# Recurrent gates of a hybrid diffusion backbone: from fp32 matmuls to three fp32r products

## The chip, the cores and the metric

One core of a Trainium2 chip runs the whole forward pass in one launch. The metric is the device time of one execution in microseconds, the median of the runs. The engines are TensorE (PE, with its weight loads as PEld), VectorE (DVE), ScalarE (ACT), GpSimd (POOL) and SyncE (SP), which issues all DMAs of this kernel.

## The reference, cut to what matters

Two layers act on 512 latent tokens and 256 context tokens of width 1024. Each layer projects its input into three head groups, mixes them, projects back, and normalises. The first group is a bidirectional RG-LRU on 384 channels; its two gates are block-diagonal linear maps of the convolved input `u`, in blocks of 64 channels:

```python
def block_diag_linear(u, w, b):
    ub = u.reshape(u.shape[:-1] + (RG_BLOCKS, RG_BLOCK))
    return jnp.einsum('blnd,nde->blne', ub, w).reshape(u.shape) + b

def rglru_scan(u, w_a, b_a, w_x, b_x, lam, h0):
    r = jax.nn.sigmoid(block_diag_linear(u, w_a, b_a))
    i = jax.nn.sigmoid(block_diag_linear(u, w_x, b_x))
    log_a = RG_C * r * jax.nn.log_sigmoid(lam)
    a = jnp.exp(log_a)
    b = jnp.sqrt(-jnp.expm1(2.0 * log_a)) * (i * u)
    ...
```

All inputs and outputs are fp32. The other two groups are a neighbourhood attention and a gated delta rule (GDN).

## The kernel before, in words

Activations lie with channels on partitions and tokens along the free dimension: 256 context columns, then 512 latent columns. A projection (`proj`, L475 to L491) makes 128 output channels: it loads two weight tiles of 128x512 fp32, and multiplies in three fp32r products, high by high, high by low and low by high, 24 matmuls of 512 columns for the latent tokens and 24 of 256 for the context tokens (in layer 1 some leave the context out). The split of a weight tile is `wsplit` (L241): a DMA into a ring of two raw buffers, a ScalarE copy into an fp32r tile `wh` (L237), and a VectorE subtraction into `wl` (L238), both in rings of four, at a raised priority. The input activations are held split as `uh` and `ul`.

The recurrent group has three units `rg(j)` (L1057) of 128 channels in each layer, each a generator whose steps are called in an order written in `CFG["rgord"]`: the projection and convolution that make `u` (tile `rgu`, two buffers); the gate path `za` with SiLU; one step for each direction `d`; and a last step with sqrt, products and scans. A direction's step does four fp32 matmuls at L1071: two gates on 512 latent columns into the PSUM tile `nS`, and two on 256 context columns into `nT`, with the weight tile `rgw`, which one DMA per layer loads whole (128x1536 fp32, 768 KB, L1117 and L1118) when the group's pool is opened. Then ScalarE takes tanh (L1073), exp (L1077) and tanh (L1078), and VectorE the product with `u` (L1080). The last step takes sqrt on ScalarE (L1083, its function table is loaded first), and on VectorE products (L1085, L1086), scans (L1088, L1090), a sum (L1093) and the gate (L1094). `tr` and `ra` have one buffer, `ti` two. The result goes to DRAM (`spill`), or for the unit that ends last straight into the split tiles `uh` and `ul` (`y_in`, L1048 and L1049); the spilled ones are read back by `y_load`.

Beside it, the w_out tiles are loaded and split (L1150, L1151), and the output projection runs at L1177 and L1213. The steps of the groups are interleaved by numbers in `CFG`; within that, a planner at build time lays down each engine's instruction order from priorities and estimated times, and every engine, and SyncE's DMA queue, runs its instructions in that fixed order. A tile's buffer is given out again once all its readers are done.

Of the kernel before, what the change touches and what calls it, by code (L numbers as in the profile page):

```python
# [5 lines left out]
F32 = mybir.dt.float32  # L6
BF16 = mybir.dt.bfloat16
F32R = mybir.dt.float32r
I32 = mybir.dt.int32
AF = mybir.ActivationFunctionType  # L10
ALU = mybir.AluOpType
# [5 lines left out]
NCTX = 256  # L17
NLAT = 512
NTOK = NCTX + NLAT
# [5 lines left out]
CC, CL = 0, 259  # L25
# [114 lines left out]
def _build(tc, I, out, dbg=None):  # L140
    nc = tc.nc
    V, S, G, T = nc.vector, nc.scalar, nc.gpsimd, nc.tensor
    pinned = [False]

    def pin(i):
        return tc.keep_in_program_order(i) if pinned[0] else i

    def dma(**kw):
        return pin(nc.sync.dma_start(**kw))
# [91 lines left out]
    def wsplit(src, n=512):  # L241
        with tc.high_priority(offset=HP):
            return split(raw(src, n), n)
# [226 lines left out]
    for l in range(DEPTH):  # L470
# [586 lines left out]
        def rg(j):  # L1057
            u = rp[0].tile([128, 772], F32, name="rgu", tag="rgu", bufs=2)
# [2 lines left out]
            z = silu_gate(proj("za", j, ctx=not last), "zs")  # L1061
            zdone.append(j)
            yield
            tr = rp[0].tile([128, 2, NTOK], F32, name="tr", tag="tr")
            ti = rp[0].tile([128, 2, NTOK], F32, name="ti", tag="ti", bufs=2)
            a = rp[0].tile([128, 2, NTOK], F32, name="ra", tag="ra")
            for d in range(2):
                for lo, n, at in ((NCTX, NLAT, CL), (0, NCTX, CC)):
                    q = ps("nT", (128, 2, 256)) if lo == 0 else ps("nS", TWO)
                    for g in range(2):  # L1070
                        T.matmul(q[:, g, :n], rp[1][:, j, d, g, :], u[:, at:at + n], start=True, stop=True)  # L1071
                    for g, o in ((0, tr), (1, ti)):
                        S.activation(o[:, d, lo:lo + n], q[:, g, :n], AF.Tanh, scale=0.5,  # L1073
                                     bias=rbh[:, 4 * j + 2 * d + g:4 * j + 2 * d + g + 1])
                L = lh[:, 2 * j + d:2 * j + d + 1]
                L2 = lq[:, 2 * j + d:2 * j + d + 1]
                S.activation(a[:, d], tr[:, d], AF.Exp, scale=L, bias=L)  # L1077
                S.activation(tr[:, d], tr[:, d], AF.Tanh, scale=L2, bias=L2)  # L1078
                for lo, n, at in ((NCTX, NLAT, CL), (0, NCTX, CC)):
                    V.scalar_tensor_tensor(ti[:, d, lo:lo + n], ti[:, d, lo:lo + n], 1.0, u[:, at:at + n],  # L1080
                                           op0=ALU.add, op1=ALU.mult)
                yield
# [9 lines left out]
            c0 = 128 * T0  # L1092
# [8 lines left out]

        P = [na_proj(hp) for hp in range(3)]
        R = [rg(j) for j in range(3)]
        rst = ExitStack()
        rp = [None, None]

        def fill():
            yield from P[0]
            for hp in range(3):
                a = na_att(hp)  # L1110
                if hp < 2:
                    yield from mix(a, P[hp + 1], CFG["mixP"])
                else:
                    yield from a
            nst.close()
            rp[0] = rst.enter_context(tc.tile_pool(name=f"rg{l}", bufs=1, **RW))
            rp[1] = rp[0].tile([128, 3, 2, 2, 128], F32, name="rgw")  # L1117
            dma(out=rp[1].rearrange("p a b c e -> p (a b c e)"), in_=I["rgw"][l])  # L1118
            for ri in CFG["rgord"][l]:
                next(R[ri] if ri < 3 else Z[ri - 3], 0)  # L1120
                yield

        Z = [zg_proj(hp) for hp in range(2)]
        g, f = gdn(), fill()
# [54 lines left out]
        op = ost.enter_context(tc.tile_pool(name=f"op{l}", bufs=1, **RW))  # L1179
# [92 lines left out]
```

## Time and profile before

| | |
|---|---|
| Runs | 886.25, 883.73, 889.57 us; median 886.25 us |
| Profiled execution | 886.25 us, span of the instructions 884.5 us |
| Mean granted TensorE clock | 0.985 of full speed |
| Gate matmuls (L1071) | 96 records for 48 matmuls, in 12 steps |

The span runs from the first to the last instruction of the profiled execution; 1.75 us lie around it. A row of TensorE counts a matmul from its start to a modelled end, and neighbouring matmuls overlap, so their spacing from start to start tells more than their durations. fp32r tiles show as f32 in TensorE's rows.

### The profile page before, as it was taken

What the parts mean: (1) busy time and instruction counts of PE and PEld (TensorE: products, weight loads), DVE (VectorE), ACT (ScalarE), POOL (GpSimd) and SP (SyncE); (2) the same over time, 40 slices, a digit from 0 to 9 for tenths busy, and PEclk for the clock granted to TensorE, in tenths of its full rate; (3) what the DMA queues carried; (4) which work ended last, traced back from release to release, by engine and by line L of the source; (5) the groups of instructions that cost most, each with busy time, mean ns of one, the idle gap of its engine ahead of it and who ended that gap; (6) DMA issues with size and microseconds to landing.
All of it is one profiled execution on the core that took longest, in us unless ns stands there. A gap on an engine that the chain in (4) does not pass through costs nothing.

```text
span 884.5 us, 17982 instructions
## 1 busy us (share of the span) xinstructions
PE 829.5 (94%) x7164; PEld 634.2 (72%) x7164; DVE 680.8 (77%) x1532; ACT 446.7 (51%) x834; POOL 28.9 (3%) x101
## 2 busy tenths in 40 slices
PE   4999999998999999999999999999899899999895
PEld 2676677776777777778677768787676777777674
DVE  2459466797997698759979665899899777877977
ACT  3354443446445245478916644545636544349922
POOL 0000000000000010100001000000000000020001
PEclk9999999999999999999999999999899999999998
DMA  8826633211121110226534172211121211131443
GB/s 311 342 72 227 234 136 132 59 37 31 60 73 62 31 38 3 88 94 205 177 132 173 51 242 89 66 49 49 37 84 60 72 47 65 50 120 57 150 147 122
DMA packets 44901, 94.58 MB, mean 107 GB/s; under 512 B 5249, under 2 KB 10241, under 8 KB 44817
## 3 DMA queue, kind: packets, MB, share of 16 engines
q1 hardware_dynamic: 44816, 93.43, 31.6%
q8 instruction: 56, 0.92, 0.4%
q14 instruction: 29, 0.23, 0.1%
HBM read 84.22 MB, written 9.19 MB: 106 GB/s over the span
## 4 chain that ended last, share of the span: by engine, by line
PE 56%; DVE 22%; ACT 10%; issue 6%; DMA 3%; POOL 1%; SPq 1%; DVEq 0%; POOLq 0%; ACTq 0%
PE pj L489 26%; PE pj L1213 3%; PE nT L985 2%; PE nT L198 2%; DVE wl L238 2%; PE x L846 2%; DVE nsb L977 2%; PE x L198 1%; PE x L1213 1%; PE gab L198 1%; PE nS L198 1%; DVE ti L1090 1%; PE nS L590 1%; ACT wh L237 1%; ACT dgc L738 1%
## 5 line engine op out<-in xcount | busy, mean ns | idle before, releaser
L489 PE MATMUL pj<-uh,wh 128*128 128x512 f32 (+1 forms) x680 | 246.2, 362 | 0.0
L489 PE MATMUL pj<-ul,wh 128*128 128x512 f32 (+1 forms) x680 | 242.8, 357 | 0.0
L489 PE MATMUL pj<-uh,wl 128*128 128x512 f32 (+1 forms) x680 | 242.2, 356 | 0.0
L489 PEld LDWEIGHTS pj<-uh,wh 128*128 128x128 f32 x680 | 129.8, 191 | 22.8 <-issue 7.3
L489 PEld LDWEIGHTS pj<-ul,wh 128*128 128x128 f32 x680 | 129.9, 191 | 16.9 <-issue 3.2
L489 PEld LDWEIGHTS pj<-uh,wl 128*128 128x128 f32 x680 | 129.9, 191 | 14.2 <-issue 0.9
L238 DVE TENSOR_TENSOR wl<-raw,wh 128x512 fp32r<-128x512 f32 (+1 forms) x106 | 71.8, 680 | 44.3 <-ACT wh L237 44.0
L237 ACT ACTIVATE wh<-raw 128x512 fp32r<-128x512 f32 (+1 forms) x106 | 65.7, 623 | 70.8 <-PE pj L489 67.6
L981 ACT ACTIVATE nsb<-nsb,mx 128x512 f32<-128x512 f32 x48 | 34.5, 720 | 30.5 <-DVE mx L979 30.1
L987 ACT ACTIVATE ptb<-nT 128x512 f32<-128x512 f32 (+1 forms) x60 | 33.4, 557 | 26.0 <-PE nT L985 25.5
L985 PE MATMUL nT<-cst,nsb 128*128 128x128 f32 x216 | 36.8, 287 | 4.9 <-ACT ptb L987 3.5
L543 DVE SCALAR_TENSOR_TENSOR cs<-xp,tph,cs 128x771 f32<-128x771 f32 (+1 forms) x36 | 35.0, 973 | 2.8 <-ACT cs L541 2.2
L985 PEld LDWEIGHTS nT<-cst,nsb 128*128 128x128 f32 x216 | 23.8, 142 | 16.5 <-ACT ptb L987 7.3
L198 PE MATMUL nT<-ptb,vt 128*64 128x128 f32 x432 | 31.1, 285 | 3.4 <-ACT ptb L987 3.4
L828 ACT ACTIVATE sb<-vtm 64x256 f32<-64x256 f32 x48 | 19.6, 413 | 23.7 <-DVE sb L839 14.0
L752 DVE TENSOR_TENSOR ln<-ln,tmp 128x60 f32<-128x60 f32 (+14 forms) x60 | 30.2, 503 | 1.2
L198 PEld LDWEIGHTS nT<-ptb,vt 128*64 128x64 f32 x432 | 23.7, 140 | 10.2 <-ACT ptb L987 9.3
L750 DVE TENSOR_TENSOR tmp<-ln 128x60 f32<-128x60 f32 (+14 forms) x60 | 30.0, 501 | 1.0
L198 PE MATMUL nS<-kT,qT 64*128 64x512 f32 (+1 forms) x180 | 26.9, 403 | 1.0 <-DVE mx L977 0.9
L1226 ACT ACTIVATE lsq<-rr,mv 128x1024 bf16<-128x1024 f32 x10 | 11.7, 1166 | 30.8 <-DVE mv L1224 30.8
L539 ACT ACTIVATE xp<-pj 128x512 f32<-128x512 f32 (+1 forms) x30 | 14.7, 488 | 21.8 <-PE pj L489 18.0
L977 DVE CUSTOM_DVE_ANT_1 nsb<-nS,bt 128x512 f32<-128x512 f32 x36 | 24.4, 685 | 1.4 <-ACT ptb L987 0.7
(300 smaller groups left out, 1668.3 us busy)
## 6 DMA issues: line engine op xcount, KB each, us to landing
raw<-in_win SPq DMA_DIRECT2D x104, 256.0 KB, 2.6
wm<-in_wmod SPq DMA_DIRECT2D x48, 512.0 KB, 5.6
raw<-in_wout SPq DMA_DIRECT2D x32, 256.0 KB, 2.8
bt<-in_rpb SPq DMA_DIRECT2D x18, 256.0 KB, 2.7
xt<-in_x SPq DMA_DIRECT2D x12, 256.0 KB, 7.8
xr<-in_x SPq DMA_DIRECT2D x12, 256.0 KB, 2.5
xpd<-xo SPq DMA_DIRECT2D x12, 256.0 KB, 2.0
yd<-zs SPq DMA_DIRECT2D x6, 384.0 KB, 3.0
```

The costliest lines, as they stand in the source:

```text
L198: return lambda: T.matmul(o, a, b, start=start, stop=stop)
L237: S.activation(h[:, :n], t[:, :n], AF.Copy)
L238: V.tensor_tensor(out=l[:, :n], in0=t[:, :n], in1=h[:, :n].bitcast(F32), op=ALU.subtract)
L489: T.matmul(q[:, :n], a[:, sl], b[:, bl_, kc, :], start=k == 0, stop=k == 23)
L543: V.scalar_tensor_tensor(o, x[:, lo_ + k:k + NCONV], taps[:, k:k + 1], o, op0=ALU.mult, op1=ALU.add)
L750: V.tensor_tensor(out=tv, in0=ln[:, :, k + 1:32, k:k + 1].to_broadcast([128, 2, n, k]), in1=ln[:, :, k:k + 1, 0:k].to_broadcast([128, 2, n ...
L752: V.tensor_tensor(out=ln[:, :, k + 1:32, 0:k], in0=ln[:, :, k + 1:32, 0:k], in1=tv, op=ALU.add)
L977: V.tensor_tensor_reduce(sb.rearrange("p (a b) -> p a b", a=2), p_[:, h2].rearrange("p (a b) -> p a b", a=2), bias, 1.0, -3e38, op0=ALU.ad ...
L981: S.activation(sb[:, 0:128 * nk], src, AF.Exp, bias=mx[:, 0, b, h2:h2 + 1], accum_out=mx[:, 1, b, h2:h2 + 1])
L985: T.transpose(pt[:, g, :], sb[:, 128 * g:128 * g + 128], ident)
L987: S.activation(t_[:, 0:nk], pt[:, 0:nk], AF.Copy)
L1213: T.matmul(q, a[:, t, kc, :], b, start=k == 0, stop=k == 23)
```

## The change

The gates' matmuls take split operands. Each unit splits its 128x512 part of the gate weights with `wsplit`, that is, through the raw, `wh` and `wl` rings of the projections, and splits `u` into two fp32r tiles `ruh` and `rul` with one buffer each, by a ScalarE copy and a VectorE subtraction for the latent and for the context columns. Each fp32 matmul becomes three fp32r ones that accumulate in PSUM. The tile `rgw` and its load are gone; the two new tiles take the same 6 KB per partition.

```diff
@@ -1061,6 +1061,11 @@
             z = silu_gate(proj("za", j, ctx=not last), "zs")
             zdone.append(j)
             yield
+            wh, wl = wsplit(I["rgw"][l][:, 512 * j:512 * j + 512])
+            uu = [rp[0].tile([128, NTOK], F32R, name="ru" + a, tag="ru" + a) for a in "hl"]
+            for lo, n, at in ((NCTX, NLAT, CL), (0, NCTX, CC)):
+                S.activation(uu[0][:, lo:lo + n], u[:, at:at + n], AF.Copy)
+                V.tensor_tensor(out=uu[1][:, lo:lo + n], in0=u[:, at:at + n], in1=uu[0][:, lo:lo + n].bitcast(F32), op=ALU.subtract)
             tr = rp[0].tile([128, 2, NTOK], F32, name="tr", tag="tr")
             ti = rp[0].tile([128, 2, NTOK], F32, name="ti", tag="ti", bufs=2)
             a = rp[0].tile([128, 2, NTOK], F32, name="ra", tag="ra")
@@ -1068,7 +1073,9 @@
                 for lo, n, at in ((NCTX, NLAT, CL), (0, NCTX, CC)):
                     q = ps("nT", (128, 2, 256)) if lo == 0 else ps("nS", TWO)
                     for g in range(2):
-                        T.matmul(q[:, g, :n], rp[1][:, j, d, g, :], u[:, at:at + n], start=True, stop=True)
+                        c0 = 256 * d + 128 * g
+                        for i, (a_, b_) in enumerate(((wh, uu[0]), (wh, uu[1]), (wl, uu[0]))):
+                            T.matmul(q[:, g, :n], a_[:, c0:c0 + 128], b_[:, lo:lo + n], start=i == 0, stop=i == 2)
                     for g, o in ((0, tr), (1, ti)):
                         S.activation(o[:, d, lo:lo + n], q[:, g, :n], AF.Tanh, scale=0.5,
                                      bias=rbh[:, 4 * j + 2 * d + g:4 * j + 2 * d + g + 1])
@@ -1102,7 +1109,7 @@
         P = [na_proj(hp) for hp in range(3)]
         R = [rg(j) for j in range(3)]
         rst = ExitStack()
-        rp = [None, None]
+        rp = [None]
 
         def fill():
             yield from P[0]
@@ -1114,8 +1121,6 @@
                     yield from a
             nst.close()
             rp[0] = rst.enter_context(tc.tile_pool(name=f"rg{l}", bufs=1, **RW))
-            rp[1] = rp[0].tile([128, 3, 2, 2, 128], F32, name="rgw")
-            dma(out=rp[1].rearrange("p a b c e -> p (a b c e)"), in_=I["rgw"][l])
             for ri in CFG["rgord"][l]:
                 next(R[ri] if ri < 3 else Z[ri - 3], 0)
                 yield
```

## Rows read from the trace of the kernel before

**Rows 1.** The page's first part: busy time of each engine, share, instructions.
```profile
PE 829.5 (94%) x7164; PEld 634.2 (72%) x7164; DVE 680.8 (77%) x1532; ACT 446.7 (51%) x834; POOL 28.9 (3%) x101
```

**Rows 2.** Chain of waits, 360 to 420 us: start, duration, what.
```profile
368.07 14.42 PE pj L489 x86
382.49 1.72 PE nS L1071 x4
384.21 0.86 PE nT L1071 x4
...
394.09 0.62 DVE zs L810 x2
```

**Rows 3.** Busy time by stretches: length, busy PE, PEld, DVE, ACT, POOL, clock, DMA.
```profile
376.00:384.00 8.00, 8.00 (x44) 6.46 (x44) 5.38 (x7) 2.14 (x5) 0.17 (x3) 1.00 0.21 57
...
395.00:417.00 22.00, 22.00 (x115) 17.82 (x115) 22.00 (x31) 19.69 (x32) 0.00 (x0) 1.00 0.67 213
...
423.00:451.00 28.00, 27.48 (x112) 20.69 (x112) 27.26 (x38) 19.29 (x28) 0.00 (x0) 1.00 0.60 195
773.00:782.00 9.00, 8.98 (x123) 6.63 (x122) 8.28 (x24) 1.88 (x4) 2.67 (x4) 1.00 0.12 38
...
792.00:824.00 32.00, 27.31 (x117) 19.88 (x116) 23.65 (x34) 29.84 (x44) 0.00 (x0) 1.00 0.33 107
824.00:854.00 30.00, 28.43 (x113) 21.88 (x111) 26.14 (x35) 19.75 (x29) 0.00 (x0) 0.94 0.43 142
```

**Rows 4.** Timeline of TensorE at layer 1's tail: start, duration, instruction, wait before.
```profile
823.55 0.50 PE L1177 MATMUL pj<-wh,uh 128*128 128x512 f32 x1 [3.13 <-ACT uh L1048]
```

**Rows 5.** Timeline of TensorE, 375 to 386 us: projections, then gate matmuls.
```profile
375.83 0.39 PE L489 MATMUL pj<-uh,wl 128*128 128x512 f32 x1
...
379.23 0.39 PE L489 MATMUL pj<-uh,wl 128*128 128x512 f32 x1
379.46 0.28 PE L489 MATMUL pj<-uh,wh 128*128 128x256 f32 x1
...
382.21 0.28 PE L489 MATMUL pj<-uh,wl 128*128 128x256 f32 x1
382.33 1.88 PE L1071 MATMUL nS<-rgu,rgw 128*128 128x512 f32 x4
...
385.14 0.40 PE L489 MATMUL pj<-ul,wh 128*128 128x512 f32 x1
```

**Rows 6.** Timeline of TensorE's weight loads, 381 us.
```profile
381.01 0.19 PEld L489 LDWEIGHTS pj<-uh,wl 128*128 128x128 f32 x1
381.13 0.19 PEld L489 LDWEIGHTS pj<-uh,wh 128*128 128x128 f32 x1
```

**Rows 7.** Timeline of ScalarE, 792 to 806 us.
```profile
792.41 0.63 ACT L1150 ACTIVATE wh<-raw 128x512 fp32r<-128x512 f32 x1 [3.60 <-DMA raw<-in_wout]
...
802.92 1.28 ACT L1083 ACT_TABLE_LOAD   x1
...
804.22 1.49 ACT L1083 ACTIVATE tr<-tr 128x1536 f32<-128x1536 f32 x1
```

**Rows 8.** Timeline of ScalarE: weight copies and copies of 768 columns.
```profile
396.68 1.14 ACT L237 ACTIVATE wh<-raw 128x512 fp32r<-128x512 f32 x2
...
427.65 1.59 ACT L1048 ACTIVATE uh<-yr 128x768 fp32r<-128x768 f32 x2
```

**Rows 9.** Timeline of VectorE: the subtractions, and a wait for the sqrt.
```profile
397.52 1.28 DVE L238 TENSOR_TENSOR wl<-raw,wh 128x512 fp32r<-128x512 f32 x2
...
418.72 0.96 DVE L1085 SCALAR_TENSOR_TENSOR tr<-ra,tr 128x768 f32<-128x768 f32 x1 [1.67 <-ACT tr L1083]
...
429.48 1.80 DVE L1049 TENSOR_TENSOR ul<-yr,uh 128x768 fp32r<-128x768 f32 x2
```

**Rows 10.** Waits of the SyncE DMA queue, 354 to 460 us: total, times, longest.
```profile
SPq L149 <- DVE wl L238: 56.9, 12, 37.4
```

## The prediction

> **What bounds the kernel now.** I read the page's totals first, then the chain of waits, then busy time by stretches, and only then single instructions. The totals name no clear owner: TensorE's matmuls cover 94% of the span, but these records overlap, so a full row does not prove that TensorE sets the pace; VectorE has 77%, ScalarE 51% [rows 1]. The reader should see in the chain that the recurrent group begins under TensorE and ends under others: from 368.07 the chain is 14.42 us of projections, then one step of gate matmuls (1.72 and 0.86 us), and at 394.09 it passes to VectorE [rows 2]. From there the stretches decide. In layer 0 VectorE is busy 22.0 of 22 us (395 to 417) and 27.26 of 28 (423 to 451); in layer 1 ScalarE is busy 29.84 of 32 us (792 to 824) and VectorE 26.14 of 30 (824 to 854) [rows 3]. In these tails three recurrent units pass through tanh, exp, sqrt and scans; TensorE looks full there too, but it is filled with the output projection and stops for 3.13 us at 823.55 until ScalarE has split a y tile [rows 4]. Before the tails the picture is the reverse: at 376 to 384 TensorE is full while ScalarE works 2.14 of 8 us [rows 3].
>
> So the change buys time on the engine that waits for the tails and pays on the two that set them.
>
> **TensorE: what the products save.** Neighbouring single-pass fp32r matmuls give the price of the new form: 16 of 128x512 begin between 375.83 and 379.23, (379.23-375.83)/15 = 0.227 us each; 24 of 128x256 between 379.46 and 382.21, 2.75/23 = 0.120 us each. The old form: the first gate matmul starts at 382.33, the second projection matmul after the step at 385.14; less the one projection matmul between, 2.81-0.23 = 2.58 us [rows 5], and the chain gives the same, 1.72+0.86 [rows 2]. One step is two gates on 512 and two on 256 columns; in the new form 2 x 3 x 0.227 + 2 x 3 x 0.120 = 2.08 us. It saves 0.50 us a step, and 2 layers x 3 units x 2 directions = 12 steps make 6.0 us of TensorE. The fp32 gate records come twice per matmul (96 for 48), so loads of weights rise from 96 to 144; a load lasts 0.19 us while loads of the neighbours start 0.12 us apart [rows 6], so they lie beside matmuls and I charge nothing; without that cover see the third rival.
>
> Of the 6.0 us only the first unit's part in layer 0 lies on the chain [rows 2]: two steps, 1.0 us at most, of which I take 0.7, since the second step can also wait for the tanh that empties its PSUM tile. In layer 1 the step after 785 hands over to ScalarE, which then stands 3.60 us for a DMA of w_out [rows 7], so nothing is gained there. The other eight steps lie in the tails, where a tile `tr` with one buffer, ScalarE's queue and VectorE decide; I count them as zero.
>
> **ScalarE and VectorE: what the splits cost.** Each of the six units gets one weight split (512 columns) and two u splits (512 and 256 columns), each an ScalarE copy and a VectorE subtraction. Prices are of instructions that follow each other: two ScalarE weight copies in 1.14 us, so 0.57 each; two 768-column copies in 1.59, so 0.80 [rows 8]. The u copy in two pieces lies between 0.80 and 2 x 0.57 = 1.14; I take 0.9, nearest to the row with the same number of columns. VectorE: 1.28/2 = 0.64 for a weight tile and 1.80/2 = 0.90 for 768 columns [rows 9], in two pieces between 0.90 and 1.28, taken 1.0. A unit costs ScalarE 0.57+0.9 = 1.5 us and VectorE 0.64+1.0 = 1.6 us. Over six units that is 9.0 and 9.6 us, more than the 6.0 that TensorE gains.
>
> Where they lie: unit 0 of layer 0 finds ScalarE at 2.14 of 8 us and VectorE at 5.38 of 8 [rows 3], hidden, zero; if that cover were gone, 1.6. Unit 0 of layer 1 falls at 773 to 782, where ScalarE has room (1.88 of 9) and VectorE little (8.28 of 9) [rows 3]; between 0 and 1.6, I take 0.5. Units 1 and 2 of layer 0 meet a full VectorE: 2 x 1.6 = 3.2 us. One gap of 1.67 us is there, before the product at 418.72, but it waits for the sqrt on ScalarE [rows 9], which the copies move back as well, so it absorbs little; between 0 and 3.2 I take 2.4. Units 1 and 2 of layer 1 meet a full ScalarE: 2 x 1.5 = 3.0 us against 2.2 idle in 32 [rows 3], most of which is waiting on others; taken 2.0. Both u tiles have one buffer, so a unit's copies wait for the last gate matmul of the unit before. That puts them between that unit's tanhs and its sqrt, in a queue that runs in order: behind them stand the exps and the sqrt, and VectorE waits for that sqrt.
>
> **Loads and the ring.** The single load of 768 KB of gate weights per layer goes, three of 256 KB come, the same bytes; nobody waited for the old one, so its removal gives zero. The new loads go through the raw ring (two buffers) and the wh/wl ring (four), and a gate weight holds its place until both of its unit's steps are over. The SyncE queue already stands 56.9 us in this stretch for VectorE to free a raw buffer [rows 10], and behind it stand w_out loads, spills and y reloads. A split needs about 0.57+0.64 = 1.2 us, 4.0 if ScalarE is at its table load and sqrt (1.28+1.49 [rows 7]). A projection needs the second half of its weights 12 x 0.227 = 2.7 us after its start, and the first half of the one before is given up 12 x 0.120 = 1.4 us ahead of its end: 4.1 us of cover, more with gate matmuls between. Just enough; I charge zero, with the second rival as the upper end and, since later loads can also relieve a busy stretch, -1 us below.
>
> **The sum.** -0.7 (TensorE) + 0 + 0.5 (units 0) + 2.4 + 2.0 (units 1 and 2) = +4.2 us. The profiled execution took 886.25 us, 1.75 more than its span of 884.5, and is itself the median of the runs, so the sum stands on that: 890.4. By its own bounds this case runs from 886.25-0.7-1 = 884.6 to 886.25+1.6+3.2+3.0 = 894.0.
>
> **Rivals.**
>
> First, TensorE sets the pace to the end. For it speaks that its row is full in 27.48 of 28 us in layer 0's last stretch [rows 3], so that any delay there may be made good. Then all 12 steps count: 886.25-6.0 = 880.2. Against it: the stop at 823.55 [rows 4], after which the next stretch has a mean granted clock of 0.94 [rows 3], that is, part of it at 1.2 instead of 2.4 GHz; saved matmul time would lengthen such stops.
>
> Second, the slow side: the ring starves. The gate weights' loads stand in SyncE's queue until a ring buffer is free, and w_out loads behind them come late. The price of one such wait is on record: 3.60 us on ScalarE, with the gates' tanh queued behind [rows 7]. If units 1 and 2 of both layers each bring one and half of it shows, 4 x 3.6 / 2 = 7.2 on top of 4.2: 897.7. It decides from the point where a w_out tile or the second half of a projection's weights lands after its user is ready.
>
> Third, a rule that speaks against three loads per gate. The rows show loads starting closer together than one lasts [rows 6]. The Trainium skill, "TensorE: Matmul & The Clock Gate", Part 3, says that LDWEIGHTS overlaps with matmuls in flight only when the row group differs, and here all use the whole array; by that rule the trace disagrees. As a mechanism of this kernel: if each of the 12 products paid its 0.19 us load, a step would take 2.08+2.28 = 4.36 instead of 2.58, 1.78 x 12 = 21 us, 907.6. The fp32r rows leave it 1 in 100.
>
> Fourth, VectorE binds from end to end. Busy shares speak for it: 77% [rows 1]. The Trainium skill, "Perfetto Trace Analysis", Identifying the Most-Contended Engine, tells one to discount matmul busy time and to look at LDWEIGHTS time, which is 72% here [rows 1]; by it the change moves work from a less to a more contended engine, and this trace's tails agree, its projection stretch does not. All six units would count: 886.25+9.6 = 895.9.
>
> **How the numbers follow.** My sum 0.56, the first rival 0.20, the second 0.15, the fourth 0.08, the third 0.01. The likeliest gives 890.4. The build's planner also lays the whole static order anew, which can move any of these by some us. The range from 879 to 900 reaches just past the first rival and the second and leaves 2 in 10 out. One per cent, 8.9 us, is about what a measurement here can tell from no change: below 877.4 lies 0.05 (more than all TensorE can save), above 895.1 lies 0.20 (most of the second and fourth, the edge of my sum), 0.75 between.
>
> **What would show it.** Right: 72 gate matmul records of each column form (144 in all) with spacing 0.227 and 0.120; steps of 2.1 us; TensorE's stops before the output projection longer than 3.13 us; sqrt of units 1 and 2 some 1 to 3 us later against the end of the projections. Wrong: if the last unit's y arrives earlier than before relative to layer start, the tails were TensorE's; if ScalarE's waits on w_out loads or the projections' waits on wl grow by several us, it was the ring; if the planner lays the tails quite differently, the sum of single prices was the wrong tool.

## The result and the profile after

The changed kernel takes 902.88 us (median of 4 runs, 902.09 to 903.91) against 886.3 us of the kernel before; the ratio is 1.0167, with a 95% interval of 1.014 to 1.0193. The forecast was 890.4 us in a range from 879 to 900, so it was too low by 12.5 us and its range ended 3 us too early. The profiled execution of the changed kernel took 902.39 us, with a span of 900.6 us and a mean granted clock of 0.974 (884.5 us and 0.985 before).

In what follows a unit's gates are tanh on L1080 (L1073 before), its products L1092 and L1093 (L1085, L1086), its scans L1095 and L1097 (L1088, L1090), its gated output L1101 (L1094), its gate matmuls L1078 (L1071). The split of `u` is L1067 (`ruh`, ScalarE) and L1068 (`rul`, VectorE), the split of w_out L1155 and L1156, the output projection L1182 and L1218.

The page's first part after, to lay beside [rows 1]:

```profile
PE 832.6 (92%) x7212; PEld 641.1 (71%) x7212; DVE 690.6 (77%) x1550; ACT 453.9 (50%) x852; POOL 29.4 (3%) x101
```

VectorE has 9.8 us more work (9.6 were forecast) and ScalarE 7.2 (9.0 forecast): the work that was added has about the size it was given. TensorE's row grows by 3.1 us, though each step shrank, as its timeline at layer 0's first step shows (to compare with [rows 5]):

```profile
383.08 0.40 PE L1078 MATMUL nS<-ruh,wh 128*128 128x512 f32 x1
...
384.25 0.39 PE L1078 MATMUL nS<-ruh,wl 128*128 128x512 f32 x1
384.48 0.28 PE L1078 MATMUL nT<-ruh,wh 128*128 128x256 f32 x1
...
385.06 0.28 PE L1078 MATMUL nT<-ruh,wl 128*128 128x256 f32 x1
385.19 0.39 PE L489 MATMUL pj<-uh,wh 128*128 128x512 f32 x1
```

The spacing is (384.25-383.08)/5 = 0.234 us for 512 columns and 0.58/5 = 0.116 us for 256, and the step lasts 385.19-383.08 = 2.11 us, as forecast. One reason for the longer row is a lower clock, shown below.

Busy time by stretches after (length, busy PE, PEld, DVE, ACT, POOL, clock, DMA share, GB/s); the first, fourth and fifth row answer to [rows 3]:

```profile
423.00:451.00 28.00, 24.96 (x108) 19.25 (x106) 22.14 (x32) 23.33 (x32) 0.00 (x0) 1.00 0.57 181
450.00:460.00 10.00, 2.87 (x5) 1.33 (x5) 9.36 (x11) 2.47 (x4) 0.00 (x0) 0.59 0.43 140
460.00:470.00 10.00, 9.71 (x32) 7.74 (x33) 4.16 (x8) 0.23 (x1) 0.00 (x0) 0.73 0.11 39
792.00:824.00 32.00, 29.45 (x157) 24.39 (x155) 22.64 (x37) 24.80 (x40) 2.81 (x7) 1.00 0.39 124
824.00:854.00 30.00, 24.82 (x111) 18.85 (x112) 27.30 (x42) 26.05 (x42) 0.00 (x0) 1.00 0.35 112
860.00:870.00 10.00, 5.24 (x15) 2.90 (x13) 8.53 (x11) 0.63 (x1) 0.00 (x0) 0.74 0.44 166
```

In the tail of layer 0 (423 to 451) the two engines that were full before now have gaps: VectorE 22.14 of 28 us where it had 27.26, TensorE 24.96 where it had 27.48. The tail ends later now, so a stretch fixed in time does not hold the same work; from 395 to the last gated output VectorE is busy 53.6 of 56 us before and 57.1 of 65 after. More work, and less of it side by side: that is the look of a chain that has got longer, not of an engine that has got fuller.

Where the 16.1 us of span went, from the times of five events in the two timelines (us; "longer by" is for the stretch since the event above):

```
                                     before     after    longer by
first gate tanh, layer 0             384.25     384.68      0.4
last gated output of layer 0         451.18     459.36      7.75
first gate tanh, layer 1             787.55     797.01      1.3
last gated output of layer 1         853.33     867.84      5.05
end of the span                      884.5      900.6       1.6
```

12.8 of the 16.1 us lie in the two tails. Each unit's first gate tanh and its sqrt cut a tail into six stretches (us, from the same timelines):

```
                                  layer 0                     layer 1
                           before  after  longer by    before  after  longer by
unit 0: tanh to sqrt         9.13  10.98     1.9        16.67  17.20     0.5
to unit 1's tanh             7.94  12.68     4.7         6.45   9.31     2.9
unit 1: tanh to sqrt        15.88  15.60    -0.3        10.83  13.17     2.3
to unit 2's tanh             8.60  12.52     3.9         9.73   6.76    -3.0
unit 2: tanh to sqrt        13.34  10.86    -2.5        11.54  12.88     1.3
to the last gated output    12.04  12.04     0.0        10.56  11.51     1.0
```

In layer 0 the largest piece lies ahead of unit 1's first tanh. TensorE and ScalarE before, then VectorE and ScalarE after:

```profile
396.99 1.88 PE L1071 MATMUL nS<-rgu,rgw 128*128 128x512 f32 x4
...
401.32 0.69 ACT L1073 ACTIVATE tr<-nS,rbh 128x512 f32<-128x512 f32 x1 [0.29 <-DVE ti L1086]
```

```profile
393.84 0.43 DVE L1068 TENSOR_TENSOR rul<-rgu,ruh 128x256 fp32r<-128x256 f32 x1
...
408.34 0.68 ACT L1080 ACTIVATE tr<-nS,rbh 128x512 f32<-128x512 f32 x1
...
435.17 1.28 ACT L1080 ACT_TABLE_LOAD   x1 [3.24 <-DVE ti L1093]
```

The step's operands are there at 394.27, but TensorE's order now has 93 projection matmuls ahead of it, and it starts at 405.19; it started at 396.99. The second piece is the last of these rows: the table load for unit 2's tanh stands 3.24 us for unit 1's last product, which VectorE's order has behind a scan and four subtractions of y; before, there was one such subtraction and no scan. In this layer every `rul` stands ahead of the scans. In the kernel with two buffers for the `u` tiles (e2 below; its trace is of the slowest of its four runs) both pieces are gone, and this tail is 3.5 us longer than before instead of 7.75.

In layer 1, 2.9 us lie ahead of unit 1's first tanh, where splits of weights stand between unit 0's products (shown at e9 below). The next 2.3 lie between that tanh and unit 1's sqrt, where `rul`'s context part stands behind unit 0's scans and TensorE waits for it, VectorE and then TensorE:

```profile
824.51 1.28 DVE L1097 TENSOR_TENSOR_SCAN ti<-ra,ti 128x512 f32<-128x512 f32 x1
...
827.22 0.42 DVE L1068 TENSOR_TENSOR rul<-rgu,ruh 128x256 fp32r<-128x256 f32 x1
```

```profile
827.69 0.39 PE L1078 MATMUL nT<-rul,wh 128*128 128x256 f32 x1 [1.19 <-DVE rul L1068]
```

Unit 2 has the same link. Before, TensorE does its first gate step 1.6 us after `u` is there (816.1):

```profile
817.68 1.88 PE L1071 MATMUL nS<-rgu,rgw 128*128 128x512 f32 x4
819.39 1.03 PE L1071 MATMUL nT<-rgu,rgw 128*128 128x256 f32 x4
```

That is 831.23-(819.39+1.03) = 10.8 us ahead of the tanh that reads it, which ScalarE runs at 831.23 while VectorE is still in unit 1's scans:

```profile
831.23 0.69 ACT L1073 ACTIVATE tr<-nS,rbh 128x512 f32<-128x512 f32 x1
```

After, the context part of the same step on TensorE, VectorE's last scan and the subtraction that follows it, and ScalarE's tanh:

```profile
839.47 0.28 PE L1078 MATMUL nT<-ruh,wh 128*128 128x256 f32 x1
846.18 0.39 PE L1078 MATMUL nT<-rul,wh 128*128 128x256 f32 x1
```

```profile
844.53 1.28 DVE L1097 TENSOR_TENSOR_SCAN ti<-ra,ti 128x512 f32<-128x512 f32 x1
845.73 0.40 DVE L1068 TENSOR_TENSOR rul<-rgu,ruh 128x256 fp32r<-128x256 f32 x1
```

```profile
847.07 0.47 ACT L1080 ACTIVATE tr<-nT,rbh 128x256 f32<-128x256 f32 x1 [2.36 <-PE nT L1078]
```

The first product runs at 839.47; the second needs `rul`, whose subtraction stands in VectorE's queue behind unit 1's scans, and runs 6.7 us later. ScalarE waits 2.36 us for it. Yet this wait is not where the layer's loss lies: from unit 1's sqrt to the last gated output the changed kernel takes 0.7 us less than the kernel before, since the first tanh of unit 2 comes 3.0 us sooner after that sqrt.

After that comes a second loss, at the end of each tail. First before, then after: TensorE's timeline where the last unit's y arrives (start, duration, instruction, wait before):

```profile
452.11 0.50 PE L1177 MATMUL pj<-wh,uh 128*128 128x512 f32 x1 [1.61 <-ACT uh L1048]
...
455.07 0.40 PE L1213 MATMUL x<-wh,ul 128*128 128x512 f32 x1
...
854.05 0.50 PE L1177 MATMUL pj<-wh,uh 128*128 128x512 f32 x1 [1.62 <-ACT uh L1048]
```

```profile
449.38 0.50 PE L1218 MATMUL x<-wh,uh 128*128 128x512 f32 x1 [0.51 <-ACT wh L1155]
455.29 0.80 PE L1218 MATMUL x<-wl,uh 128*128 128x512 f32 x1 [5.41 <-DVE wl L1156]
...
460.29 0.80 PE L1182 MATMUL pj<-wh,uh 128*128 128x512 f32 x1 [2.00 <-ACT uh L1048]
...
465.53 0.40 PE L1218 MATMUL x<-wh,uh 128*128 128x512 f32 x1
...
864.30 0.51 PE L1218 MATMUL x<-wl,uh 128*128 128x512 f32 x1 [2.97 <-DVE wl L1156]
...
868.55 0.80 PE L1182 MATMUL pj<-wh,uh 128*128 128x512 f32 x1 [1.25 <-ACT uh L1048]
```

Before, the last y is waited for once in each layer, 1.61 and 1.62 us (the stop of 3.13 us in [rows 4] lies earlier in the tail); now there are two stops in each, 5.41 and 2.00 us, 2.97 and 1.25. TensorE runs out of output-projection matmuls that don't need the last y (the rest wait for a w_out split at the end of VectorE's queue) and stands for most of 449.9 to 460.3. After it, 12 matmuls of the projection take 465.53-460.29 = 5.24 us; the same 12 took 455.07-452.11 = 2.96 us before. The granted clock says why: it is 1.00 from 450 to 470 before, and 0.59 and 0.73 after:

```profile
450.00:460.00 10.00, 8.39 (x37) 6.31 (x36) 5.33 (x10) 0.84 (x1) 0.00 (x0) 1.00 0.21 70
460.00:470.00 10.00, 9.79 (x47) 7.73 (x46) 7.75 (x17) 4.13 (x10) 1.50 (x2) 1.00 0.34 120
860.00:870.00 10.00, 10.00 (x44) 8.06 (x43) 6.97 (x19) 2.49 (x4) 2.25 (x4) 1.00 0.30 105
```

The last of these three rows of before is layer 1's; after, that stretch has 0.74, and the same 12 matmuls take 4.30 us (868.55 to 872.85) instead of 2.91. So 2.3 and 1.4 us are paid after y is there, by matmuls of which all in layer 0 and the first half in layer 1 run at 1.2 instead of 2.4 GHz. Of the 2.3 us, the stretch up to layer 1's first tanh shows 1.3.

SyncE's queue waits no longer for raw buffers than before [rows 10]; the same row of its waits, 354 to 460 us, after:

```profile
SPq L149 <- DVE wl L238: 52.8, 11, 37.3
```

### The profile page after: what moved, and what is told of

It is laid out like the page before. It is cut to its first block, busy times and chain, and to the rows that moved or that the text cites. A ratio compares the mean times of both kernels' runs of the same rounds, so it can differ in the third digit from the quotient of the medians.

```text
span 900.6 us, 18124 instructions
## 1 busy us (share of the span) xinstructions
PE 832.6 (92%) x7212; PEld 641.1 (71%) x7212; DVE 690.6 (77%) x1550; ACT 453.9 (50%) x852; POOL 29.4 (3%) x101
## 5 line engine op out<-in xcount | busy, mean ns | idle before, releaser
L238 DVE TENSOR_TENSOR wl<-raw,wh 128x512 fp32r<-128x512 f32 (+1 forms) x112 | 76.0, 681 | 44.3 <-ACT wh L237 43.8
L237 ACT ACTIVATE wh<-raw 128x512 fp32r<-128x512 f32 (+1 forms) x112 | 69.6, 624 | 73.2 <-PE pj L489 69.5
L1218 PE MATMUL x<-wl,uh 128*128 128x512 f32 x40 | 17.2, 430 | 9.1 <-DVE wl L1156 8.9
```

The lines of the kernel that those rows point to most:

```text
L237: S.activation(h[:, :n], t[:, :n], AF.Copy)
L238: V.tensor_tensor(out=l[:, :n], in0=t[:, :n], in1=h[:, :n].bitcast(F32), op=ALU.subtract)
L1218: T.matmul(q, a[:, t, kc, :], b, start=k == 0, stop=k == 23)
```

## The experiments

Ratios are to the kernel before, run on the same chip, with 95% intervals; a microsecond behind one is its distance from 1 times 887 us. Each median is of 4 to 12 runs.

**Which part of the changed kernel, if taken back, brings the time back?** The first four leave the computation as it is. e1 gives raw, high and low tile of the gate weights one buffer of their own, off the projections' rings:

```diff
-            wh, wl = wsplit(I["rgw"][l][:, 512 * j:512 * j + 512])
+            with tc.high_priority(offset=HP):
+                wh, wl = split(raw(I["rgw"][l][:, 512 * j:512 * j + 512], tag="gr", bufs=1, pl=rp[0]), 512, rp[0], ("gwh", "gwl"), 1)
```

> The changed kernel with the gate weights in tiles of their own (one raw, one wh, one wl, outside the projections' rings). Ring theory (the gate weights' place in the rings makes unit 1's first gate step of layer 0 wait behind a projection): that step returns ahead of the 48 projection matmuls and the 7.4 us lost in layer 0's tail go, 894 to 896 us. Buffer theory (the u copies of a unit wait for the last gate matmul of the unit before, since ruh and rul have one buffer): no gain, 900 to 905. Work theory (9.0 and 9.6 us more on ScalarE and VectorE are the whole cost): no gain, 901 to 904.

Measured: 909.18 us, 1.0253 (1.0231 to 1.0274), slower than the change itself. e2 gives the u tiles two buffers:

```diff
-            uu = [rp[0].tile([128, NTOK], F32R, name="ru" + a, tag="ru" + a) for a in "hl"]
+            uu = [rp[0].tile([128, NTOK], F32R, name="ru" + a, tag="ru" + a, bufs=2) for a in "hl"]
```

> The changed kernel with two buffers each for ruh and rul, the weights still in the rings. Buffer theory: unit 1's first gate step of layer 0 runs ahead of the third unit's projection, layer 0's loss of 7.4 us goes, layer 1's of about 5 stays: 893 to 897 us. Ring theory: 900 to 904. Work theory: unchanged, 901 to 904.

Measured: 897.75 us, 1.0133 (1.01 to 1.0166). About 5 us of median come back; by the ratios it is 3.0, and the two intervals overlap. e3 puts the copies and subtractions of `u` into a `with tc.high_priority(offset=HP):`, and e4 does both:

> The changed kernel with the u copies and subtractions at the raised priority of the weight splits, one buffer. Queue-place theory (in layer 1 the 256-column pieces stand behind the sqrt on ScalarE and the scans on VectorE, and the gates' context halves wait for them): layer 1's 5 us go, layer 0's 7.4 stay: 896 to 900 us. Work theory: 901 to 904, since the same instructions run.

> Both: two buffers for ruh and rul and the raised priority. Buffer and queue-place theories together: 888 to 892 us, which is what the sum of single prices gave (890.4). Work theory: 900 to 904. Ring theory: 898 to 903.

Measured: e3 901.84 us, 1.0166 (1.0131 to 1.0201), nothing; e4 897.93 us, 1.012 (1.0096 to 1.0143), what e2 gives, here 0.47%, 4.2 us, with intervals that hardly touch. A second buffer helps; a raised priority does not. Yet in e3's layer 1 every `rul` stands ahead of the scans (unit 2's at 827.52 and 828.12, unit 1's first scan at 838.17), and unit 1's stretch from tanh to sqrt is back at 11.2 us (10.8 before, 13.2 in the changed kernel). Other stretches take up what that gives: the tail is still 4.4 us longer than before. So the place of `rul` behind the scans is not the whole of the loss.

**One part alone, on the kernel before.** e5 has only the three products: `u` leaves the convolution rounded to fp32r, the weights are rounded once per layer, and each fp32 matmul becomes three equal products, with the tanh's scale divided by 3.

```diff
-                        T.matmul(q[:, g, :n], rp[1][:, j, d, g, :], u[:, at:at + n], start=True, stop=True)
+                    for g, i in ((0, 0), (0, 1), (0, 2), (1, 0), (1, 1), (1, 2)):
+                        T.matmul(q[:, g, :n], rp[1][:, j, d, g, :], ur[:, at:at + n], start=i == 0, stop=i == 2)
```

> The kernel before with the TensorE part alone: the convolution writes u rounded to fp32r, three ScalarE copies per layer round the gate weights early, and each gate is three equal fp32r products (tanh divides by three). The low parts of u and of the weights are left out, and with them all splits inside the units. If TensorE's saving lies mostly off the path (my step of -0.7): 885 to 888 us. If TensorE sets the pace in the tails: 881 to 883.

e6 has only the u copies and subtractions, with the fp32 matmul reading `ruh`; e7 only the gate weights through `wsplit` and the rings, with the fp32 matmul reading `wh`:

```diff
-                        T.matmul(q[:, g, :n], rp[1][:, j, d, g, :], u[:, at:at + n], start=True, stop=True)
+                        T.matmul(q[:, g, :n], rp[1][:, j, d, g, :], uu[0][:, lo:lo + n].bitcast(F32), start=True, stop=True)
...
+                        T.matmul(q[:, g, :n], wh[:, 256 * d + 128 * g:256 * d + 128 * g + 128].bitcast(F32), u[:, at:at + n], start=True, stop=True)
```

> The kernel before with the u split alone: both tiles are written, the fp32 gate matmuls read the high part, the low part is not used. Work theory (the added instructions stand in the queues on the way from one unit's sqrt to the next unit's tanh): 5 to 6 us slower than before, 892 to 894. Buffer theory without work: the order of the gate steps is that of before, so no more than +2, 886 to 889.

> The kernel before with the weight splits alone: gate weights through the projections' rings, fp32 gate matmuls on u with the high part of the weights, the low part is not used. Work theory: six splits of 0.57 and 0.64 us, some of them hidden: 888 to 890. Ring theory in a weaker form (a place in the ring delays the loads of w_out and of y): 893 to 897.

Measured: e5 885.3 us, 0.997 (0.9947 to 0.9992), -2.7 us; e6 891.08 us, 1.0029 (1.0005 to 1.0054), +2.6 us; e7 896.17 us, 1.0086 (1.0052 to 1.012), +7.6 us. Together that is 7.5 of the 14.8 us that the ratio of the whole change makes. e8 gives `tr` two buffers in the changed kernel, since before it was the tile whose one buffer seemed to order the tails:

> The changed kernel with two buffers for tr, so that a unit's tanh need not wait for the last product of the unit before. If the way from unit to unit leads through tr, 3 to 6 us come back: 897 to 900. If the engines are simply full, nothing comes back: 901 to 904.

Measured: 904.16 us, 1.0181 (1.0152 to 1.021): nothing comes back, `tr` is not it.

**What of the ring part costs: the loads, the ring places, or the work?** e9 is e7 with the gate weights loaded whole as before and split from there into the `wh` and `wl` ring; e10 splits them into tiles of their own (the line shown); e11 makes e9's edit in the changed kernel:

```diff
+            rp[1] = rp[0].tile([128, 1536], F32, name="rgw")
+            dma(out=rp[1], in_=I["rgw"][l])
...
+            with tc.high_priority(offset=HP):
+                wh, wl = split(rp[1][:, 512 * j:512 * j + 512], 512, rp[0], ("gwh", "gwl"), 1)
```

> The kernel before with the gate weights loaded whole by one DMA, as before, and split unit by unit into the wh and wl ring of the projections; the gates stay fp32 matmuls, on the high part alone (the low part of the gate weights is unused). Against the ring-only kernel (896.2, +7.6 us over before), this takes the gate weights out of the raw ring and out of the three loads. If the loads cost (raw buffers, SyncE's queue): only the split work stays, some +3.6, 891.5 us. If the places in the wh and wl ring cost: it stays near 896. If neither, but the split work on ScalarE and VectorE in the tails: it stays near 896 here and in the next kernel too.

> As the last kernel, but the split gate weights lie in a wh and wl tile of their own with one buffer, so neither ring of the projections is touched; fp32 gates on the high part alone. What is left is the split work: 6 x 0.57 us of ScalarE and 6 x 0.64 us of VectorE. If a ring or a load cost the 7.6 us of the ring-only kernel: 888 to 892. If the split work itself, laid into full queues, costs them: 896.

> The changed kernel with the gate weights loaded whole by one DMA as in the kernel before, and split into the wh and wl ring. If the three loads through the raw ring cost: some 4 us come back, 898 to 899. If the ring places, the split work or the order of the gate steps cost: 902 to 904.

Measured: e9 894.87 us, 1.009 (1.0057 to 1.0122); e10 890.17 us, 1.0036 (1.0015 to 1.0058); e11 902.61 us, 1.0158 (1.0121 to 1.0195). The three loads cost nothing. The split work costs 3.2 us, near the 3.6 of its rows, and the places in the `wh` and `wl` ring the rest, 0.9 - 0.36 = 0.54%, 4.8 us (the intervals of the two together leave 1.4 to 8.2). VectorE's and ScalarE's timelines in layer 1's tail show how; first e9, then e10:

```profile
809.46 0.96 DVE L1087 SCALAR_TENSOR_TENSOR tr<-ra,tr 128x768 f32<-128x768 f32 x1 [2.10 <-ACT tr L1085]
810.34 0.68 DVE L238 TENSOR_TENSOR wl<-raw,wh 128x512 fp32r<-128x512 f32 x1
810.94 0.95 DVE L1088 TENSOR_TENSOR ti<-ti,tr 128x768 f32<-128x768 f32 x1
811.81 0.68 DVE L238 TENSOR_TENSOR wl<-rgw,wh 128x512 fp32r<-128x512 f32 x1
...
814.95 0.93 DVE L1088 TENSOR_TENSOR ti<-ti,tr 128x768 f32<-128x768 f32 x1
```

```profile
815.96 1.28 ACT L1075 ACT_TABLE_LOAD   x1 [1.83 <-DVE ti L1088]
```

```profile
810.35 1.82 DVE L1088 TENSOR_TENSOR ti<-ti,tr 128x768 f32<-128x768 f32 x2
```

```profile
812.25 1.28 ACT L1075 ACT_TABLE_LOAD   x1
```

With the gate weights in the ring, the split of a projection's weights (`wl<-raw`) and the next gate weights (`wl<-rgw`) stand between unit 0's products; in e10 both products run on end. The products are done at 815.88 instead of 812.17, and the next unit's table load, which waits 1.83 us for them in e9, comes 3.7 us later; e9 was 1.4 us later already at its layer's first tanh (790.92 and 789.56), so 2.3 of the 4.8 us are lost here. The last two splits of projection weights run at 796.30 and 799.54 in e10 (VectorE is busy 4.9 of 8 us from 793 to 801) and at 803.16 and 810.34 in e9 (8.0 of 8 from 810 to 818): the ring moved splits out of a stretch where VectorE had room into the one where it is the chain. The changed kernel's timeline has the same two splits there, at 816.61 and 818.08. The stretch from unit 0's sqrt to unit 1's first tanh is 2.9 us longer than before in ten of the eleven kernels here whose gate weights go through the ring (not in e8, where `tr` has two buffers and the next stretch grows by 6.9), and at most 0.3 longer in the eight where they don't.

**Is it the place of unit 1's gate step in the order?** In the changed kernel's layer 0, TensorE's order has unit 1's first gate step behind 93 projection matmuls on end, where the kernel before has 45, that step, and 48 more. e12 writes the order of steps so that it stands between them again, with one buffer:

```diff
-CFG = {..., "rgord": [[0, 1, 0, 0, 0, 1, 0, 2, 1, 1, 2, 2, 2, 1, 2], ...
+CFG = {..., "rgord": [[0, 1, 0, 0, 0, 1, 0, 1, 2, 1, 2, 2, 2, 1, 2], ...
```

> The changed kernel with layer 0's written order of steps changed at one place, so that unit 1's first gate step stands ahead of unit 2's projection again, as in the kernel before; ruh and rul keep one buffer. If the place of that step in the order cost what two buffers gave back: 897.5 to 898.5. If it was the wait for the single buffer itself, which now stops TensorE in front of that projection: 902 or more.

Measured: 902.72 us, 1.0161 (1.0123 to 1.02). The place of this step alone gives nothing back. In e12's trace unit 1's first tanh comes 1.0 us late instead of 4.7, but its sqrt comes another 4.2 us late after it. e2, whose order has the step in the same place, gave 5 us of median: there only 1.8 are lost in that stretch. So the second buffer gives more than the place of one step; what makes the sqrt late in e12 was not separated.

**Which pair of parts makes the other half?** e13 is the changed kernel with fp32 matmuls (u copies and ring weights, no products). e17 has products and u copies with the weights rounded once and off the rings; e18 has products and ring weights on a rounded `u`. Both leave a low part out and do the first product a second time in place of the one that would read it. First e17's products, then e18's:

```diff
+                        for i, b_ in enumerate((uu[0], uu[1], uu[0])):
+                            T.matmul(q[:, g, :n], rp[1][:, j, d, g, :], b_[:, lo:lo + n], start=i == 0, stop=i == 2)
...
+                        for i, a_ in enumerate((wh, wl, wh)):
+                            T.matmul(q[:, g, :n], a_[:, c0:c0 + 128], ur[:, at:at + n], start=i == 0, stop=i == 2)
```

> The changed kernel with all its splits, tiles and loads, and only the products as before: one fp32 matmul on the high parts (the low parts of u and of the weights are made and not used). If the parts add up and only the three products bring the other half (their three operands bind the step to the last subtraction and move the order): 887 + 2.6 + 7.6 = 897. If the other half comes from u copies and ring weights standing together: 902.7 + 2.7 = 905.

> The kernel before with the u copies and subtractions and with three products on them (high, low, high part of u), the gate weights only rounded once per layer, off both rings (their low part is left out, and the third product stands in for it). If the products' loss comes from their operands, since a step now waits for the subtraction on VectorE behind tail work and for the u tile's one buffer: 895, like the changed kernel without its ring part. If products and u copies add up: 887 - 2.7 + 2.6 = 887.

> The kernel before with the gate weights split through the projections' rings and three products on them (high, low, high part of the weights), on a u that the convolution leaves rounded (no u copies, the low part of u is left out). If the products' loss comes from the ring, since the low part of the weights is now an operand too: 900. If products and ring weights add up: 887 + 7.6 - 2.7 = 892. If both pairs add up, only all three together make the other half, through the order: then the granted clock stays at 1.00 from 450 to 470 us here and falls only in kernels where TensorE runs out of work before the last unit's y.

Measured: e13 894.86 us, 1.0083 (1.0059 to 1.0107); e17 900.08 us, 1.0146 (1.0119 to 1.0173); e18 893.76 us, 1.006 (1.0037 to 1.0082). With these the table of parts is complete (per cent over the kernel before; "sum" adds the single parts):

```
                        measured     sum
products                  -0.30
u copies                  +0.29
ring weights              +0.86
u copies + ring           +0.83     +1.15
products + ring           +0.60     +0.56
products + u copies       +1.46     -0.01
all three                 +1.67     +0.85
```

One pair makes it: the products and the u copies cost nothing as a sum and 1.46%, 13.0 us, together. The half widths of the three intervals behind that difference are 0.22 to 0.27, so it stands far outside them. Once it is there, the ring adds 0.2%, within the noise of the two (0.4%): both losses are waits in the same tails and partly cover each other. In e17's layer 1, unit 1 takes 4.0 us longer from tanh to sqrt than before, and unit 2's first tanh comes 4.0 us later after unit 1's sqrt; in the changed kernel, with the ring's 2.9 us ahead of them, it is 2.3 us longer and 3.0 us sooner. In e17's unit 1, ScalarE waits 2.03 us for the gate matmuls that read `rul`'s context part, made behind unit 0's scans. What joins the two parts is, by the code, that the products read `rul` as well, made on VectorE; e6 and e13 make it, but their gates read `ruh` alone.

The fall of the clock at the end of layer 0's tail does not belong to this pair. First the ring alone (e7), then products and u copies (e17):

```profile
450.00:460.00 10.00, 7.67 (x25) 5.25 (x24) 6.56 (x10) 0.84 (x1) 0.00 (x0) 0.83 0.65 219
```

```profile
450.00:460.00 10.00, 9.73 (x42) 7.39 (x41) 8.21 (x12) 0.84 (x1) 0.00 (x0) 1.00 0.43 154
860.00:870.00 10.00, 4.65 (x11) 2.97 (x10) 7.41 (x10) 0.63 (x1) 0.00 (x0) 0.64 0.24 79
```

From 450 to 460 the granted clock is 0.83 in e5, e7, e9 and e18, with the products alone or the ring, and 1.00 in e6, e10, e13 and e17; so what e18's expectation says of the clock missed. From 860 to 870 it is 0.64 in e17 and 1.00 in the seven others.

**And what takes it away?** e14 is the changed kernel with gate weights in high and low tiles of their own (e1 without its own raw tile); e15 adds a second buffer for `ruh` alone (the last two lines); e16 adds e3's priority to that.

```diff
-            wh, wl = wsplit(I["rgw"][l][:, 512 * j:512 * j + 512])
+            with tc.high_priority(offset=HP):
+                wh, wl = split(raw(I["rgw"][l][:, 512 * j:512 * j + 512]), 512, rp[0], ("gwh", "gwl"), 1)
-            uu = [rp[0].tile([128, NTOK], F32R, name="ru" + a, tag="ru" + a) for a in "hl"]
+            uu = [rp[0].tile([128, NTOK], F32R, name="ru" + a, tag="ru" + a, bufs=2 if a == "h" else 1) for a in "hl"]
```

> The changed kernel with the split gate weights in a wh and wl tile of their own, one buffer each; the raw loads stay in the projections' raw ring. If the ring places cost in the whole change what they cost alone: 902.7 - 4.7 = 898. If the single buffers of gate weights and u then hold each other up, as with the own raw tile (909): 903 to 909.

> As the last one, and ruh with two buffers (rul keeps one). If ring places (4.7 us) and the wait for the u tile (5 us with two buffers for both) are two separate costs: 902.7 - 9.7 = 893. If they are one and the same wait seen twice: 897 to 898.

> As the last one, and the u copies and subtractions at the raised priority of the weight splits, so that TensorE's order in layer 1 comes near that of the kernel before (35 of 48 projection matmuls no longer pulled between the gates). If what is left is the split work less TensorE's gain: 887 + 3.1 + 2.6 - 2.7 = 890. If the raised copies push other work of ScalarE and VectorE back by as much: 893 as the one before it.

Measured: e14 905.16 us, 1.0188 (1.0154 to 1.0222); e15 895.21 us, 1.0082 (1.0059 to 1.0105); e16 895.48 us, 1.0074 (1.0049 to 1.0099). Between e14 and e15 the only edit is one more buffer for `ruh`, and 1.06%, 9.4 us, come back. Unit 2 of layer 1 in e14, VectorE and then ScalarE:

```profile
842.36 1.28 DVE L1098 TENSOR_TENSOR_SCAN ti<-ra,ti 128x512 f32<-128x512 f32 x1
844.74 0.68 DVE L1069 TENSOR_TENSOR rul<-rgu,ruh 128x512 fp32r<-128x512 f32 x1
845.94 0.42 DVE L1069 TENSOR_TENSOR rul<-rgu,ruh 128x256 fp32r<-128x256 f32 x1
```

```profile
848.27 0.69 ACT L1081 ACTIVATE tr<-nS,rbh 128x512 f32<-128x512 f32 x1
```

The same in e15, ScalarE and then VectorE:

```profile
820.49 0.94 ACT L1068 ACTIVATE ruh<-rgu 128x512 fp32r<-128x512 f32 x2 [0.39 <-DVE rgu L543]
...
837.64 0.69 ACT L1081 ACTIVATE tr<-nS,rbh 128x512 f32<-128x512 f32 x1
```

```profile
827.52 1.02 DVE L1069 TENSOR_TENSOR rul<-rgu,ruh 128x512 fp32r<-128x512 f32 x2
...
839.00 1.27 DVE L1098 TENSOR_TENSOR_SCAN ti<-ra,ti 128x512 f32<-128x512 f32 x1
```

With two buffers `ruh` is copied when `u` is ready, `rul` follows ahead of unit 1's scans, and the gates' tanh (837.64) runs beside them, as in the kernel before. With one buffer the copy can't start before unit 1's last gate matmul (828.24), and the order has it behind unit 1's sqrt as well, at 836.96; `rul` lands behind the scans, and the tanh comes 848.27-(842.36+1.28) = 4.6 us after their end. From unit 1's sqrt to unit 2's first tanh e14 takes 13.7 us, e15 6.5 and the kernel before 9.7. But `rul` is not the only thing that e14's tanh has ahead of it: ScalarE's order also has the copy of a reloaded y there, which stands 4.58 us for its DMA (4.63 us at the same place in e17), and the gate matmuls end only 0.29 us after ScalarE is through with that and the next copy. What the buffer changes is the whole order that is laid around the wait, not one wait.

e16 says the same: its raised priority takes unit 1's `rul` in layer 1 out from behind unit 0's scans (809.21; 820.98 in e15), unit 1's stretch from tanh to sqrt falls from 15.8 to 12.0 us, and the time stays where it was.

No version that computes the whole of the reference beats the kernel before.

## Why the prediction was wrong, point by point

**TensorE's saving: right in size per step, small in worth.** The step measures 2.11 us (2.08 forecast). Alone the products give 2.7 us back; the interval, 0.7 to 4.7 us, just takes in the 0.7 that was forecast. The first rival, all 6.0 us on the path, falls.

**The price of the splits as work: right.** Split work of the weights 3.2 us (e10) and copies of `u` 2.6 us (e6) make 5.8 us, against 0.5 + 2.4 + 2.0 = 4.9 in the sum; each of the two has an interval of about 2 us to either side.

**The step that failed: "Both u tiles have one buffer, so a unit's copies wait for the last gate matmul of the unit before. That puts them between that unit's tanhs and its sqrt".** The prediction saw the wait and then priced it as work, 1.5 us of ScalarE and 1.6 of VectorE for a unit. The place of the copies it had right: in layer 0 they run at 391.95 and 417.77, ahead of the sqrts at 395.66 and 423.94. What it left out is who then waits. Before, a unit's gates needed `u`, which has two buffers, and TensorE could do them 10 us ahead of their tanh; after, they need `ruh` and `rul`, which can't be begun until the unit before is through its gate matmuls, and the whole static order of gate matmuls, tanhs and products is laid around that. The pair of products and u copies costs 13.0 us for work that sums to nothing, and a second buffer of one tile gives 9.4 us back where the weights have their own tiles (5 us of median, 3.0 by the ratios, in the changed kernel as it is). So much the runs show.

By which wait it costs is read in timelines, and it is not the same one everywhere. In layer 0 it is unit 1's gate step behind 93 projection matmuls (4.7 us) and a product behind a scan and y subtractions (3.9, of which 2.5 come back later), with every `rul` ahead of the scans. In layer 1 `rul` stands behind the scans, 2.3 us in unit 1; the wait of 2.36 us in unit 2 costs nothing on balance. That `rul`'s place on VectorE carries the loss is not shown: e3 and e16 put it ahead of the scans and the time stays. A kernel with products that leaves `rul` unread was not run.

**"Just enough; I charge zero" for loads and ring: wrong by 4.8 us taken alone.** Right in it: the three loads (e9, e11). Wrong: the ring places. The second rival had the ring costing, at 897.7, and the ring alone does give 896.2, near it by chance; its mechanism, waits on w_out loads multiplied, isn't there. Those waits fell from 5.2 us in all to 2.4; in the kernels with the ring alone they rose a little, to 7.4 (e7) and 7.1 (e9), but e10, without the ring, has 6.0. The part of the cost that was found is the splits' new place in VectorE's order.

**The third rival falls.** The Trainium skill, "TensorE: Matmul & The Clock Gate", Part 3, has two statements: its list says that weight loads overlap matmuls in flight only for another row group, while its mechanism also lets a load that targets the background weight buffer go ahead of them. Here the gates' 144 loads follow each other on the whole array, and the products still start 0.234 and 0.116 us apart; the trace disagrees with the first and not with the second.

**The fourth rival falls.** VectorE's added 9.8 us do not show one to one: the same work with fp32 gates (e13) costs 7.4 us, of which 4.8 are the ring places.

**What wasn't in the sum: the clock.** The longer chain leaves TensorE without work ahead of the last y, and the matmuls that follow run at half the clock: 2.3 + 1.4 us, of which not all reaches the end.

**The signs that it named.** The records and steps came as said. The stop before the last y's matmuls is over 3.13 us in layer 0 alone (5.41; 2.97 in layer 1). The sqrt of units 1 and 2 come later against the first tanh of their layer by 6.3 and 7.8 us in layer 0 and 5.7 and 4.1 in layer 1, not 1 to 3: the sign for "the sum of single prices was the wrong tool", and so it was.

**What stays open.** e15 and e16 take away the ring places and most of the wait, and still cost 0.8% where the parts sum to 0.35% (-0.30 + 0.29 + 0.36). Some 4 us are left, about as much as the noise of the four ratios together (0.46%), so it may be nothing. In e15's layer 1 unit 1's `rul` still stands behind unit 0's scans, and its stretch from tanh to sqrt is 5.0 us longer than before; in e15 the granted clock also falls to 0.66 from 450 to 460, where kernels with the products or the ring alone have 0.83. These were not separated. Nor was the path in layer 0 tested by an edit that moves only the product or only the y subtractions.

## What to carry to other kernels

An operand that is newly made on another engine is a new edge in the graph before it is a cost: ask where in that engine's order its maker will stand, and who then waits, ahead of asking how long it takes. And a wait that a trace shows is not yet the loss: cut the time into stretches between the same events before and after, and see which of them grew. A scratch tile with one buffer between stages that used to overlap through a tile with two undoes the overlap; count the buffers of every tile on the new edge. And a long-lived tile put into a short-lived ring moves every later user of that ring, perhaps into the one stretch that has no room.

## What the runs showed of the hardware that was not expected

TensorE's granted clock fell to 1.2 GHz after stops that the order makes (the mean clock of the four runs is 0.973 to 0.977): after a stretch with 2.87 us of matmuls in 10, the projection's matmuls started 0.43 us apart until 465.15 and 0.23 us apart from 465.53. Weight loads of 144 products in place of 96 fp32 gate records left no trace in TensorE's spacing.
